# Layer 0's FFN, last F-tile: the context tokens' output groups and norms between the block products, head 0's weight remainders and half of the rope tables on VectorE

## The chip, the cores and the metric

One core of a Trainium2 chip runs the whole kernel. The metric is the device time of one execution in microseconds (us), as the median of several runs. The engines are TensorE (PE; its weight loads are PEld), VectorE (DVE), ScalarE (ACT), GpSimd (POOL) and the queue of SyncE (SP), which issues most transfers.

## The reference, cut to what matters

Two transformer layers over 512 latent tokens and 256 context tokens of width 1024. Each layer is a mixer (attention) and a SwiGLU FFN, each behind an RMS norm with a scale and shift, and each added to the stream through a gate row. The change is at the end of layer 0's FFN and the start of layer 1's mixer:

```
def _swiglu(h, w_in, w_out):
    gate, up = jnp.split(h @ w_in, 2, axis=-1)
    return (jax.nn.silu(gate) * up) @ w_out

x = x + gx2 * _swiglu(_rms(x, norm_ffn_w[l]) * (1.0 + scx2) + shx2, ffn_w_in[l], ffn_w_out[l])
ctx = ctx + gc2 * _swiglu(_rms(ctx, norm_ffn_w[l]) * (1.0 + scc2) + shc2, ffn_w_in[l], ffn_w_out[l])
# layer 1 (differential attention):
hx = _rms(x, norm_mix_w[l]) * (1.0 + scx1) + shx1      # the same for ctx
q, k, v = jnp.split(hx @ w_in, [qs, 2 * qs], axis=-1)  # q, k normed, and turned by rope for latent tokens
```

The FFN's hidden width is 2816, 22 F-tiles of 128.

## The kernel before, in words

Every fp32 matmul is done in three passes of the reduced type fp32r: each operand is split into a rounded part (hi, a cast on ACT) and a remainder (lo, a subtraction on DVE or POOL), and hi x hi, hi x lo, lo x hi are summed in PSUM. Names that end in h and l are these two parts: `wbh`/`wbl` blocks of FFN input weights, `wdh`/`wdl` output ("down") weights, `hdh`/`hdl` hidden rows, `wih`/`wil` layer 1's input weights, `hT` and `hTc` the normed tokens of the latents and the context, transposed.

Tokens are in six tiles of 128: 0 to 3 are latent, 4 and 5 context; `x0` to `x5` are their stream rows. `CTX_FIRST` is the order 4, 5, 0, 1, 2, 3.

`ffn_mixed` is layer 0's FFN. Its F-tiles f = 2 to 10 go through `by_blocks`. For the latents an F-tile is a fast 2 x 2 block scheme of seven products (r2, r1, r3, a11, a12, a22, r4; a product is 12 matmuls of 256 columns into `pu` or `pg`), whose weight blocks r1 to r4 are sums of the weights' four quarters (`ws`, made on POOL from the loaded `wr`). For the context the same tile takes plain gate and up products of the quarters (`gate_up`, 2 x 24 matmuls into `cgu`). `hi` and `lo` split the next weight blocks, in the order of the list `names`; the lo parts of r1 and r2 are on POOL, the others on DVE. Between the products stand groups: a group is the down product of one token tile and half of the 1024 outputs (9 matmuls of 512 columns into `dps` for three F-tiles), added to `x` by DVE. The context's groups of F-tiles 8 to 10 and the latents' all stand after the last F-tile, in the order CTX_FIRST.

What an earlier phase put into `x` was saved to DRAM. `gate(i)` makes a gate row: a transpose (`gps`), a copy (`grow`) on DVE, two DMAs. `resumed(t, eng)` loads a token tile's saved rows (`xr`) into one of two shared buffers ("raw"), multiplies `x` by the gate row and adds `xr`, on the engine given. `residual` multiplies a finished group by the gate row and adds it to `x`, both on DVE. `done(t)` is `norm_steps`: a square on ACT, an rsqrt and a scaling on POOL (`nh`), eight transposes on PE (`npt`), eight affine steps on DVE and ACT in turns (`nhc`), the split into `hT` or `hTc`.

Layer 1 works head by head. `in_proj1` loads a head's weights in four units through the raw buffers (`wir`), splits them (`by_pieces` is the subtraction in three pieces on POOL) and projects the six token tiles (`inps`, 24 matmuls each); `rotate_all` applies the rope tables `rt`, which `head_tables` makes on POOL; `kpt` and `qpt` are transposes of keys and queries. The split weights have five buffers and a head needs four.

Engines run their queues in order. The order is set by a list scheduler that models time, except in `ffn_mixed`, where `Pinned` engines keep the order in which the code is written, and where `tc.issue_after` holds an instruction behind another.

Of the kernel before, what the change touches and what calls it, by code (L numbers as in the profile page):

```python
# [18 lines left out]
P = 128  # L19
D = 1024  # L20
# [42 lines left out]
def backbone(es: ExitStack, tc: tile.TileContext, x, c, ctx, c_ctx, mod_w, mod_b, norm_mix_w, norm_ffn_w,  # L63
# [98 lines left out]
    def rsqrt(ss, n, inv, tag):  # L162

        r = small.tile([P, n], F32, name="rs_" + tag, tag="rs_" + tag)
        nc.gpsimd.tensor_scalar(r, ss, inv, EPS, ALU.mult, ALU.add)
        nc.gpsimd.tensor_tensor(r, r, neghalf[:, :n], ALU.pow)
        return r
# [78 lines left out]
    def norm_steps(t, xt, l, f, pool, tags=(("nh", 2), ("nhc", 2)), room=None):  # L246
# [8 lines left out]
        nc.scalar.activation(h, xt, AF.Square, accum_out=ss)  # L255
        r = rsqrt(ss, 1, 1.0 / D, "n")
        nc.gpsimd.tensor_scalar(h, xt, r, 1.0, ALU.mult, ALU.mult)
        yield
        hc = hc() if callable(hc) else hc
        hi, lo = tile_T(0, t), tile_T(1, t)  # L260
        for g in range(2):
            pt = tr_tile("npt", [P, 4, P])
            for k in range(4):
                nc.tensor.transpose(pt[:, k, :], h[:, 4 * g + k, :], ident)
            for k in range(4):
                kk = 4 * g + k
                a, c = aff[l][:, f, kk, i:i + 1], modc[l][:, 3 * f, kk, i:i + 1]
                if k % 2:
                    nc.scalar.activation(hc[:, kk, :], pt[:, k, :], AF.Identity, bias=c, scale=a)
                else:  # L270
                    nc.vector.tensor_scalar(hc[:, kk, :], pt[:, k, :], a, c, ALU.mult, ALU.add)
            ks = slice(4 * g, 4 * g + 4)
            nc.scalar.copy(hi[:, ks], hc[:, ks])
            nc.vector.tensor_sub(lo[:, ks], hc[:, ks], f32(hi[:, ks]))
# [51 lines left out]
    def head_tables(pool, wq, wk, nq, nk, w, rp):  # L326
# [10 lines left out]
        for j, h0, m in ((0, 0, nq), (1, nq, nk)):  # L337
            nc.vector.tensor_copy(wc[:, h0:h0 + m], bc(w[:, 0, j, :], 1, m))
            for i in range(2):
                wj = bc(bc(w[:, i, j, :], 1, m), 1, 2)  # L340
                for u in range(2):
                    nc.gpsimd.tensor_tensor(tb[u][:, :, i, h0:h0 + m], bc(rp[:, 2 * u:2 * u + 2, i, :], 2, m), wj,
                                            ALU.mult)
# [45 lines left out]
    def project(ps, t, ws, c0, c1):  # L389

        hs = [tile_T(j, t) for j in range(2)]
        for k in range(KT):
            whi, wlo = ws[k // 2]
            a, b = whi[:, k % 2, c0:c1], wlo[:, k % 2, c0:c1]
            nc.tensor.matmul(ps, hs[0][:, k, :], a, start=k == 0, stop=False)  # L395
            nc.tensor.matmul(ps, hs[0][:, k, :], b, start=False, stop=False)  # L396
            nc.tensor.matmul(ps, hs[1][:, k, :], a, start=False, stop=k == KT - 1)  # L397
# [174 lines left out]
    def in_proj1(h, tabs, wp, st, wh, qp):  # L572
        wc, tb = tabs
        ws = []
        for u in range(4):
# [5 lines left out]
            ws.append(unit(wh, views, [P, 2, 384], 5, "wi", None if h < 2 and u % 2 else by_pieces))  # L581
# [5 lines left out]
        for t in CTX_FIRST:  # L587
# [4 lines left out]
            with behind(nc.tensor) if h == 0 and t >= NTX else ExitStack():  # L592
                project(ps, t, ws, 384 - n, 384)
# [593 lines left out]
    def ffn_mixed(xs, w_down, w_up, fp, turn_over, new_rows, done, after):  # L1187
# [144 lines left out]
        names = ("r2", "r1", "r3", "a11", "a12", "a22", "a21", "r4")  # L1332

        class Weights:

            def __init__(self, f):
# [8 lines left out]
                todo.extend((self, n) for n in names)  # L1345
# [239 lines left out]
        def by_blocks(f, w, nxt, after, last, own):  # L1585
# [34 lines left out]
            if f == NF - 1:  # L1620
                gates[0] = gate(0, lambda *a, **kw: fp.tile(*a, tag="t1h", **kw))
# [22 lines left out]
            if f == NF - 1:  # L1644
# [39 lines left out]
            if f == NF - 1:  # L1684
                end(back[0])
                back[2] = resumed(2, pool)
                end(back[2])
# [9 lines left out]
            if f == NF - 1:  # L1697
                end(back[1])
                back[3] = resumed(3, pool)
                end(back[3])  # L1700
# [21 lines left out]

        w, nxt = w2, w3
        for f in range(2, NF):
# [206 lines left out]
    def done0(t):  # L1931
# [6 lines left out]
        return norm_steps(t, xs[t], 1, 0, None, room=room)  # L1938
# [216 lines left out]
```

## Time and profile before

| | us |
|---|---|
| median of 3 runs (1761.33 to 1769.43) | 1764.95 |
| the profiled execution | 1762.82 |
| its span, first to last instruction | 1760.9 |
| PE busy / POOL busy / DVE busy | 1672.6 / 1049.4 / 1192.4 |
| layer 0's last F-tile: first block product | 947.1 |
| layer 1, head 0: first projection matmul | 999.8 |

Times of instructions are us from the start of the span. In a row of the profile the line is that of kernel.py; the pinned instructions of the FFN all have one line, L765 (the wrapper), so they are told apart by their tiles. A group's row ends in "busy us, mean ns of one | idle time of the engine before them, and what ended it".

### The profile page before, as it was taken

The numbers are of one execution on the slowest core, as the hardware profiler recorded it, in microseconds if no ns is written. First come the engines' busy times: TensorE is split into PE (matmuls) and PEld (weight loads), VectorE is DVE, ScalarE is ACT, GpSimd is POOL, SyncE is SP. The second block draws the span as 40 slices with busy tenths as digits, with TensorE's granted clock in tenths as the row PEclk, the third lists the DMA queues.
The fourth block names the chain that finished last, engine by engine and source line by source line (L and its number), as shares of the span: only waits on it lengthen the run. The fifth ranks groups of instructions, "written<-read, shape, count | busy, mean of one in ns | idle before, by whom it ended". The sixth has DMA issues, their size and how long they took to land.

```text
span 1760.9 us, 30531 instructions
## 1 busy us (share of the span) xinstructions
PE 1672.6 (95%) x11322; PEld 1484.8 (84%) x11322; DVE 1192.4 (68%) x2181; ACT 915.1 (52%) x2030; POOL 1049.4 (60%) x1337
## 2 busy tenths in 40 slices
PE   5999999989899999999999889999998999999998
PEld 3887787667799998899989789999986788999997
DVE  4775555444768767877787765666665488777777
ACT  6556565533436555555553565666665355444441
POOL 2753332422647877788776766667773247777770
PEclk8999999999999999999999999999999999999999
DMA  9212233314343544454543311111122325333332
GB/s 311 63 44 73 82 99 101 128 49 124 104 132 120 157 155 144 133 166 146 155 126 125 123 37 37 36 38 37 48 94 84 96 73 167 94 94 102 108 96 96
DMA packets 206836, 184.79 MB, mean 105 GB/s; under 512 B 17056, under 2 KB 191712, under 8 KB 206688
## 3 DMA queue, kind: packets, MB, share of 16 engines
q1 hardware_dynamic: 205760, 180.55, 33.6%
q8 instruction: 89, 1.46, 0.3%
q10 hardware_dynamic: 928, 2.30, 0.3%
q14 instruction: 59, 0.48, 0.1%
HBM read 173.36 MB, written 9.46 MB: 104 GB/s over the span
## 4 chain that ended last, share of the span: by engine, by line
PE 69%; DVE 7%; POOL 7%; ACT 5%; DMA 5%; issue 3%; SPq 1%; ACTq 0%; POOLq 0%; DVEq 0%
PE dps L765 15%; PE pg L765 11%; PE pu L765 9%; PE cgu L765 5%; PE inps L395 3%; PE inps L396 3%; PE inps L397 3%; PE av L546 2%; PE sc L501 2%; PE ops L718 2%; POOL wil L286 2%; PE ops L720 2%; PE ops L719 2%; PE ppt L528 2%; PE av L666 1%
## 5 line engine op out<-in xcount | busy, mean ns | idle before, releaser
L765 DVE TENSOR_TENSOR x<-x,dps 128x512 f32<-128x512 f32 x268 | 176.4, 678 | 24.5 <-PE dps L765 24.0
L765 POOL TENSOR_TENSOR wbl<-ws,wbh 128x256 fp32r<-128x256 f32 x152 | 122.6, 837 | 105.0 <-PE pu L765 54.0
L765 PE MATMUL dps<-wdh,hdh 128*128 128x512 f32 x434 | 174.8, 403 | 8.1 <-DVE x L765 4.9
L765 PE MATMUL pg<-hT,wbh 128*128 128x256 f32 (+1 forms) x944 | 176.2, 284 | 2.4 <-DVE pg L765 1.6
L765 PE MATMUL dps<-wdl,hdh 128*128 128x512 f32 x434 | 172.2, 397 | 0.0
L765 PE MATMUL dps<-wdh,hdl 128*128 128x512 f32 x434 | 171.7, 396 | 0.3 <-DVE hdl L765 0.3
L765 ACT ACTIVATE modw<-modw,cols 128x256 f32<-128x256 f32 x256 | 109.4, 498 | 114.2 <-DMA modw<-in_mod_w_dram 103.2
L765 PEld LDWEIGHTS pg<-hT,wbh 128*128 128x128 f32 x944 | 150.8, 188 | 11.8 <-DVE pg L765 1.8
L765 POOL TENSOR_TENSOR modw<-modw 128x512 f32<-128x512 f32 (+1 forms) x96 | 119.7, 1247 | 64.9 <-ACT modw L765 59.2
L765 POOL TENSOR_TENSOR ws<-wr 128x256 f32<-128x256 f32 x152 | 145.4, 977 | 17.6 <-DMA wr<-in_ffn_w_in_dram 13.8
L395 PE MATMUL inps<-wih,hT 128*128 128x384 f32 x384 | 133.2, 347 | 0.9 <-ACT qkv L595 0.6
L765 PE MATMUL pg<-hT,wbl 128*128 128x256 f32 (+1 forms) x472 | 133.7, 283 | 0.0
L397 PE MATMUL inps<-wih,hT 128*128 128x384 f32 x384 | 131.1, 341 | 0.0
L396 PE MATMUL inps<-wil,hT 128*128 128x384 f32 x384 | 130.9, 341 | 0.0
L765 DVE TENSOR_TENSOR wbl<-wr,wbh 128x512 fp32r<-128x512 f32 x142 | 121.5, 859 | 5.9 <-ACT wbh L765 5.4
L765 PE MATMUL cgu<-hTc,wbh 128*128 128x256 f32 x640 | 114.2, 279 | 0.0
L765 ACT CAST wbh<-ws 128x512 fp32r<-128x512 f32 x152 | 87.3, 623 | 43.5 <-PE pg L765 31.6
L765 ACT CAST wbh<-wr 128x512 fp32r<-128x512 f32 x142 | 87.1, 619 | 37.3 <-PE pg L765 21.0
L765 PEld LDWEIGHTS cgu<-hTc,wbh 128*128 128x128 f32 x640 | 99.9, 188 | 3.4 <-issue 0.4
L765 PEld LDWEIGHTS dps<-wdh,hdh 128*128 128x128 f32 x434 | 81.9, 189 | 23.8 <-DVE x L765 8.4
L765 PEld LDWEIGHTS dps<-wdh,hdl 128*128 128x128 f32 x434 | 82.0, 189 | 20.2 <-DVE hdl L765 0.7
L765 PEld LDWEIGHTS dps<-wdl,hdh 128*128 128x128 f32 x434 | 82.2, 189 | 9.5
(388 smaller groups left out, 5270.7 us busy)
## 6 DMA issues: line engine op xcount, KB each, us to landing
modw<-in_mod_w_dram SPq DMA_DIRECT2D x108, 512.0 KB, 4.3
wr<-in_ffn_w_in_dram SPq DMA_DIRECT2D x84, 512.0 KB, 5.1
wdr<-in_ffn_w_out_dram SPq DMA_DIRECT2D x44, 512.0 KB, 3.7
wir<-in_od_w_in_dram SPq DMA_DIRECT2D x96, 128.0 KB, 2.3
x<-in_x_dram SPq DMA_DIRECT2D x8, 512.0 KB, 8.8
wir<-in_ev_w_in_dram SPq DMA_DIRECT2D x16, 256.0 KB, 2.8
wor<-in_ev_w_out_dram SPq DMA_DIRECT2D x8, 512.0 KB, 3.6
out_dram<-x SPq DMA_DIRECT2D x8, 512.0 KB, 2.6
```

What stands on the lines that cost most here:

```text
L286: nc.gpsimd.tensor_sub(lo[c], raw[c], hi[c])
L395: nc.tensor.matmul(ps, hs[0][:, k, :], a, start=k == 0, stop=False)
L396: nc.tensor.matmul(ps, hs[0][:, k, :], b, start=False, stop=False)
L397: nc.tensor.matmul(ps, hs[1][:, k, :], a, start=False, stop=k == KT - 1)
L501: nc.tensor.matmul(sc[:, s0:s0 + c1 - c0], q, kT[:, j, c0:c1], start=j == 0, stop=bool(j and last))
L528: nc.tensor.transpose(pt[:, h, :], Pt[h][:, cs], ident)
L546: mm = nc.tensor.matmul(av[64 * j:64 * j + 64, :], vv[:, vt[kc], :], P4[:, j::2, kc * P:(kc + 1) * P], start=i == 0, stop=i == nk - 1)
L666: nc.tensor.matmul(av, PT[:, a, :], vv[:, vt[kc], :], start=kc == 0, stop=kc == NT - 1)
L718: nc.tensor.matmul(ps, ohi[:, k, :], a, start=k == first, stop=False)
L719: nc.tensor.matmul(ps, ohi[:, k, :], b, start=False, stop=False)
L720: self.at = nc.tensor.matmul(ps, olo[:, k, :], a, start=False, stop=k == last)
L765: return tc.keep_in_program_order(op(*args, **kw))
```

## The change

The last F-tile leaves `by_blocks` for a function of its own, `last_tile`. There the context's gate and up come first, so that its hidden rows are ready early; the four context groups stand between the block products, each followed by its residual on DVE; tile 4's whole norm and the scaling of tile 5 stand before product r4. Gate row 0 is made after product r1; x0's saved rows are taken in on POOL and not on DVE, x1's on DVE, in the code behind r4. The list of weight blocks has another order for this tile. After it the latents' groups follow in the order 0 to 3, with two more PSUM banks in turn. The norms behind the FFN are pinned too.

In layer 1 all four units of head 0 are split on DVE (before: two on POOL); head 1's units 1 and 2 get two buffers in another pool; head 1's context projections may be issued after head 0's tile 1; four of the eight rope table products are on DVE.

The diff, cut to its core:

```diff
+    def norm_steps(t, xt, l, f, pool, tags=(("nh", 2), ("nhc", 2)), room=None,
+                   engs=(nc.tensor, nc.vector, nc.scalar, nc.gpsimd)):
...
+        def table(u, eng):
+            for j, h0, m in parts:
+                for i in range(2):
+                    eng.tensor_tensor(tb[u][:, :, i, h0:h0 + m], bc(rp[:, 2 * u:2 * u + 2, i, :], 2, m),
+                                      bc(bc(w[:, i, j, :], 1, m), 1, 2), ALU.mult)
+
+        table(0, nc.vector)
+        with tc.high_priority(-150):
+            table(1, nc.gpsimd)
...
-            ws.append(unit(wh, views, [P, 2, 384], 5, "wi", None if h < 2 and u % 2 else by_pieces))
+            pool, n = (wo, 2) if h == 1 and u in (1, 2) else (wh, 5)
+            ws.append(unit(pool, views, [P, 2, 384], n, "wi", None if h == 0 or h == 1 and u % 2 else by_pieces))
...
-            with behind(nc.tensor) if h == 0 and t >= NTX else ExitStack():
-                project(ps, t, ws, 384 - n, 384)
+            with tc.issue_after(first_head[0].ins) if h == 1 and t >= NTX else ExitStack():
+                mm = project(ps, t, ws, 384 - n, 384, Pinned(nc.tensor) if h == 0 and t >= NTX else nc.tensor)
+            if h == 0 and t == 1:
+                first_head.append(mm)
...
         names = ("r2", "r1", "r3", "a11", "a12", "a22", "a21", "r4")
+        last_names = ("a11", "a12", "a21", "a22", "r2", "r1", "r3", "r4")
...
-                todo.extend((self, n) for n in names)
+                todo.extend((self, n) for n in (names if f < NF - 1 else last_names))
...
-            if f == NF - 1:
-                gates[0] = gate(0, lambda *a, **kw: fp.tile(*a, tag="t1h", **kw))
...
-                for i, eng in ((0, dve), (1, dve)):
-                    back[i] = resumed(i, eng)
-                    next(back[i])
...
+        def ctx_group(t, n):
+            ps = down_bank()
+            for f in fs:
+                down_part(ps, f, t, n, f == fs[0], f == fs[-1])
+            yield
+            acc = xs[t][:, n * 512:(n + 1) * 512]
+            dve.tensor_mul(ps, ps, gates[1][:, n * 512:(n + 1) * 512])
+            dve.tensor_add(acc, acc, ps)
+            if n:
+                norms.append(done(t, (pe, dve, act, pool)))
+                next(norms[-1])
+
+        def last_tile(f, w, last):
+            t = Tile(f, w)
+            dn = down(f)
+            next(dn)
+            hidden_tiles(f)
+            t.gate_up(0)
+            next(last)
+            hi()
+            lo()
+            t.gate_up(1)
+            rest = hidden(f, SEQ, TOK, t.both[:, 0], t.both[:, 1], ctx_room("sgc"))
+            next(rest)
+            end(last)
+            next(rest)
+            next(dn)
+            end(rest)
+            t.product("r2")
+            end(dn)
+            t.product("r1")
+            gates[0] = gate(0, lambda *a, **kw: fp.tile(*a, tag="t1h", **kw))
+            back[0], back[1] = resumed(0, pool), resumed(1, dve)
+            for i in range(2):
+                next(back[i])
+            gs = [ctx_group(t, n) for t in CTX_FIRST[:2] for n in range(2)]
+            t.product("r3")
+            next(gs[0])
+            t.product("a11")
+            end(gs[0])
+            t.four()
+            end(back[0])
+            next(gs[1])
+            t.product("a12")
+            end(gs[1])
+            dve.tensor_add(t.a, t.a, t.q)
+            next(gs[2])
+            t.product("a22")
+            end(gs[2])
+            dve.tensor_add(t.e, t.e, t.u)
+            next(gs[3])
+            end(gs[3])
+            back[2] = resumed(2, pool)
+            end(back[2])
+            end(norms.pop(0))
+            t.product("r4")
+            end(back[1])
+            dve.tensor_add(t.c, t.c, t.v)
+            last = hidden(f, 0, SEQ, t.ps[1], t.ps[0], t.quv[:, :SEQ])
+            next(last)
+            back[3] = resumed(3, pool)
+            end(back[3])
+            return last
...
-        order = [(t, n) for t in CTX_FIRST for n in range(2)]
+        last = last_tile(NF - 1, w, last)
+        order = [(t, n) for t in range(NTX) for n in range(2)]
...
-            ps = open_[i] if i < 4 else acc_tile("dps", one=i % 2)
+            ps = open_[i] if i < 4 else new_bank(i)
```

How the instructions stand now, at three places. POOL, in F-tiles 9 and 10, before. (`wbl` from `ws` are the lo parts of r2 and r1, two pieces each; the `x4` and `x5` rows are the context's saved rows being taken in; `g1` is the context's gate row.)

```order
L765 TENSOR_TENSOR ws_10927<-wr_10605,wr_10607 128x256 x2
L765 TENSOR_TENSOR wbl_10944<-ws_10850,wbh_10943 128x256 x2
L765 TENSOR_TENSOR wbl_10965<-ws_10818,wbh_10964 128x256 x2
L765 TENSOR_TENSOR ws_11018<-wr_10605,ws_10850 128x256 x2
L765 TENSOR_TENSOR x4_4682<-x4_4682,g1_11014 128x1024
L765 TENSOR_TENSOR x4_4682<-x4_4682,xr_11016 128x1024
L765 TENSOR_TENSOR x5_4763<-x5_4763,g1_11014 128x1024
L765 TENSOR_TENSOR x5_4763<-x5_4763,xr_11080 128x1024
```

POOL there now:

```order
L779 TENSOR_TENSOR ws_10927<-wr_10605,wr_10607 128x256 x2
L779 TENSOR_TENSOR ws_11016<-wr_10605,ws_10850 128x256 x2
L779 TENSOR_TENSOR x4_4682<-x4_4682,g1_11012 128x1024
L779 TENSOR_TENSOR x4_4682<-x4_4682,xr_11014 128x1024
L779 TENSOR_TENSOR x5_4763<-x5_4763,g1_11012 128x1024
L779 TENSOR_TENSOR x5_4763<-x5_4763,xr_11078 128x1024
L779 TENSOR_TENSOR wbl_11083<-ws_10850,wbh_11082 128x256 x2
L779 TENSOR_TENSOR wbl_11101<-ws_10818,wbh_11100 128x256 x2
L779 TENSOR_TENSOR x0_4046<-x0_4046,g0_11265 128x1024
```

The lo parts of r2 and r1 have moved behind the four operations on `x4` and `x5`, and x0 comes to POOL.

DVE before, at the end of the last F-tile: the last products' sums (`pg`, `pu`), x0 and x1 taken in among them, then the hidden rows (`hdl`).

```order
L765 TENSOR_TENSOR pg_11164<-pg_11164,quv_11239 128x256
L765 TENSOR_TENSOR x0_4046<-x0_4046,g0_11202 128x1024
L765 TENSOR_TENSOR x0_4046<-x0_4046,xr_11223 128x1024
L765 TENSOR_TENSOR pu_11163<-pu_11163,quv_11239 128x256
L765 TENSOR_TENSOR x1_4203<-x1_4203,g0_11202 128x1024
L765 TENSOR_TENSOR x1_4203<-x1_4203,xr_11225 128x1024
L765 TENSOR_TENSOR cgu_11247<-sgc_11272,cgu_11247 128x256
L765 TENSOR_TENSOR hdl_11246<-cgu_11247,hdh_11245 128x256
L765 TENSOR_TENSOR pg_11164<-pg_11164,quv_11239 128x256
L765 TENSOR_TENSOR pu_11163<-quv_11239,pu_11163 128x512
L765 TENSOR_TENSOR hdl_11246<-pu_11163,hdh_11245 128x512
```

DVE there now, from the second lo half of tile 4's norm (`hTc1`) to the hidden rows:

```order
L779 TENSOR_TENSOR hTc1_4657<-nhc_11340,hTc0_4656 128x4x128
L779 TENSOR_SCALAR nhc_11340<-npt_11408,aff1_109,modc1_107 128x128 x2
L779 TENSOR_TENSOR hTc1_4657<-nhc_11340,hTc0_4656 128x4x128
L779 TENSOR_TENSOR x1_4203<-x1_4203,g0_11265 128x1024
L779 TENSOR_TENSOR x1_4203<-x1_4203,xr_11269 128x1024
L779 TENSOR_TENSOR pg_11164<-pg_11164,quv_11307 128x256
L779 TENSOR_TENSOR pu_11163<-quv_11307,pu_11163 128x512
L779 TENSOR_TENSOR hdl_11168<-pu_11163,hdh_11167 128x512
L779 TENSOR_SCALAR nhc_11386<-npt_11470,aff1_109,modc1_107 128x128
L302 TENSOR_TENSOR wil_11700<-wir_11695,wih_11699 128x768
```

x1 now stands directly ahead of the last sum on `pg`, behind tile 4's norm, and the first weight remainder (`wil`) follows the hidden rows.

DVE right after this, before: the residuals of the first four groups, all of them the context's.

```order
L402 TENSOR_TENSOR dps_11353<-dps_11353,g1_11014 128x512
L402 TENSOR_TENSOR dps_11354<-dps_11354,g1_11014 128x512
L403 TENSOR_TENSOR x4_4682<-x4_4682,dps_11353 128x512
L402 TENSOR_TENSOR pu_11355<-pu_11355,g1_11014 128x512
L403 TENSOR_TENSOR x4_4682<-x4_4682,dps_11354 128x512
L402 TENSOR_TENSOR pg_11356<-pg_11356,g1_11014 128x512
L403 TENSOR_TENSOR x5_4763<-x5_4763,pu_11355 128x512
L403 TENSOR_TENSOR x5_4763<-x5_4763,pg_11356 128x512
```

And now, the latents' (PSUM bank `pu` is free again after the last row, tile 1's first half being in `pu_11441`):

```order
L411 TENSOR_TENSOR dps_11439<-dps_11439,g0_11265 128x512
L779 TENSOR_SCALAR nhc_11386<-npt_11470,aff1_109,modc1_107 128x128
L412 TENSOR_TENSOR x0_4046<-x0_4046,dps_11439 128x512
L411 TENSOR_TENSOR dps_11440<-dps_11440,g0_11265 128x512
L412 TENSOR_TENSOR x0_4046<-x0_4046,dps_11440 128x512
L411 TENSOR_TENSOR pu_11441<-pu_11441,g0_11265 128x512
L302 TENSOR_TENSOR wil_11708<-wir_11703,wih_11707 128x768
L779 TENSOR_TENSOR hTc1_4657<-nhc_11386,hTc0_4656 128x4x128
L779 TENSOR_SCALAR nhc_11386<-npt_11481,aff1_109,modc1_107 128x128
L411 TENSOR_TENSOR pg_11442<-pg_11442,g0_11265 128x512
L302 TENSOR_TENSOR wil_11716<-wir_11711,wih_11715 128x768
L412 TENSOR_TENSOR x1_4203<-x1_4203,pu_11441 128x512
```

Two weight remainders, a norm's remainder and two affine steps stand among the residuals.

More of the change, by code (lines that the diff above doesn't have):

```diff
@@ L160, in backbone, with rsqrt @@
     sel2 = cst[:, C_S2:C_S2 + 2]
-    def rsqrt(ss, n, inv, tag):
+    def rsqrt(ss, n, inv, tag, eng=nc.gpsimd):
         r = small.tile([P, n], F32, name="rs_" + tag, tag="rs_" + tag)
-        nc.gpsimd.tensor_scalar(r, ss, inv, EPS, ALU.mult, ALU.add)
-        nc.gpsimd.tensor_tensor(r, r, neghalf[:, :n], ALU.pow)
+        eng.tensor_scalar(r, ss, inv, EPS, ALU.mult, ALU.add)
+        eng.tensor_tensor(r, r, neghalf[:, :n], ALU.pow)
         return r
@@ L268, in norm_steps @@
                 if k % 2:
[L269 removed]
+                    act.activation(hc[:, kk, :], pt[:, k, :], AF.Identity, bias=c, scale=a)
                 else:
[L271 removed]
+                    dve.tensor_scalar(hc[:, kk, :], pt[:, k, :], a, c, ALU.mult, ALU.add)
             ks = slice(4 * g, 4 * g + 4)
[L273 to L274 removed]
+            act.copy(hi[:, ks], hc[:, ks])
+            dve.tensor_sub(lo[:, ks], hc[:, ks], f32(hi[:, ks]))
     def norm_hT(*args, **kw):
@@ L1721, in by_blocks @@
             return last, own
+        fs = tuple(range(NF - 3, NF))
+        norms = []
+        def ctx_group(t, n):
[60 more added lines that the diff above has]
+            return last
         w, nxt = w2, w3
-        for f in range(2, NF):
+        for f in range(2, NF - 1):
             after = Weights(f + 2) if f + 2 < NF else None
@@ L1727, in ffn_mixed, with new_bank @@
             w, nxt = nxt, after
-        fs = tuple(range(NF - 3, NF))
-        order = [(t, n) for t in CTX_FIRST for n in range(2)]
-        open_ = [p_1.tile([P, 512], F32, name="dps", tag=f"acc{i}") for i in range(2)] + \
-            [banks.tile([P, SEQ], F32, name=n, tag=n) for n in ("pu", "pg")]
+        last = last_tile(NF - 1, w, last)
+        order = [(t, n) for t in range(NTX) for n in range(2)]
+        def new_bank(i):
+            return p_1.tile([P, 512], F32, name="dps", tag=f"acc{i % 2}") if i in (0, 1, 6, 7) else \
+                banks.tile([P, SEQ], F32, name=("pu", "pg")[i % 2], tag=("pu", "pg")[i % 2])
+        open_ = [new_bank(i) for i in range(4)]
         for ps, (t, n) in zip(open_, order):
@@ L1735, in ffn_mixed @@
         end(last)
-        norms = []
+        end(norms.pop(0))
         for i, (t, n) in enumerate(order):
-            ps = open_[i] if i < 4 else acc_tile("dps", one=i % 2)
+            ps = open_[i] if i < 4 else new_bank(i)
             for f in fs[2 * (i < 4):]:
                 down_part(ps, f, t, n, f == fs[0], f == fs[-1])
-            residual(xs[t], ps, gates[t >= NTX], n)
+            residual(xs[t], ps, gates[0], n)
             if n:
```

46 lines of the change are left out of this document (18 added, 28 removed).

## The prediction

> **What bounds the kernel now.** I read the head and busy shares of the page first, then PE's waits from 947 us (the start of layer 0's last F-tile) to the third head of layer 1, then a table of stretches of that time.
>
> ```profile
> span 1760.9 us, 30531 instructions
> PE 1672.6 (95%) x11322; PEld 1484.8 (84%) x11322; DVE 1192.4 (68%) x2181; ACT 915.1 (52%) x2030; POOL 1049.4 (60%) x1337
> ```
>
> TensorE is the bound over the whole span, so a change that keeps its matmuls can win only where it stands still. Stretches: length, then busy us of PE, PEld, DVE, ACT, POOL, then PE's granted clock.
>
> ```profile
> 947.00:964.00 17.00, 16.16 (x136) 15.97 (x136) 13.70 (x20) 4.20 (x8) 7.96 (x3) 1.00 0.37 125
> 979.00:1000.00 21.00, 16.47 (x76) 12.84 (x75) 17.46 (x32) 13.94 (x29) 14.81 (x19) 0.92 0.52 169
> 1014.00:1032.00 18.00, 15.03 (x88) 13.95 (x87) 12.67 (x28) 13.55 (x33) 12.23 (x22) 0.91 0.03 8
> 1032.00:1045.00 13.00, 10.45 (x66) 9.27 (x65) 6.15 (x14) 7.97 (x20) 9.45 (x17) 0.87 0.39 111
> 1074.00:1084.00 10.00, 7.09 (x45) 6.54 (x43) 2.53 (x6) 4.20 (x13) 8.32 (x16) 0.83 0.29 83
> ```
>
> PE idles 0.8, 4.5, 3.0, 2.6 and 2.9 us here, 13.8 in all, and where it idles the clock falls too. In the second row DVE is busy 17.5 of 21 us: it is the engine that PE waits for. The waits by name (total, times, longest):
>
> ```profile
> PE npt L264 <- ACT nhc L269: 3.6, 2, 2.3
> PE kpt L622 <- ACT o L269: 2.4, 1, 2.4
> PE inps L396 <- POOL wil L286: 2.1, 1, 2.1
> PE inps L395 <- ACT wih L299: 1.2, 1, 1.2
> PE pg L765 <- DVE quv L765: 0.8, 1, 0.8
> ```
>
> The first is the tail of the FFN, the second tile 2's norm behind head 0's projections, the wil and wih rows the weights of heads 1 and 2.
>
> **The change, part by part.** TensorE's own work is as before; its pieces in the chain (start, us):
>
> ```profile
> 851.44 1.44 PE pu L765 x12
> 852.88 1.39 PE dps L765 x6
> 862.73 2.80 PE cgu L765 x24
> ```
>
> *The last tile's start.* Gate and up of the context now come first, at the place of r2's first matmul (947.1, below): two of 2.80, to 952.7. Then r2 and r1 are wanted, but their lo parts stand on POOL behind context's four row operations, which wait for gate row 1.
>
> ```profile
> 936.21 0.27 DVE L765 COPY grow<-gps 8x128 f32<-8x128 f32 x1
> 941.80 2.39 POOL L765 TENSOR_TENSOR x<-x,g 128x1024 f32<-128x1024 f32 x1 [2.82 <-DMA g<-gmem]
> 949.88 2.75 POOL L765 TENSOR_TENSOR x<-x,xr 128x1024 f32<-128x1024 f32 x1
> L765 POOL TENSOR_TENSOR wbl<-ws,wbh 128x256 fp32r<-128x256 f32 x4 | 2.9, 754 | 0.6 <-PE dps L765 0.6
> ```
>
> The four end at 952.6; the copy of the row starts about 1.2 later than at 936.21, since DVE now does two lo parts ahead of it, so they end at 953.8, and the first half of r2's lo 0.75 later, 954.5. r2's third matmul wants it at 952.9, so PE waits 1.6 (0 if DVE has slack for the two, 2.5 if they also collide with POOL). The 0.8 behind DVE quv goes, since a group now runs while q is copied; I keep it as slack within these bounds.
>
> *The groups between products.* Where PE stood and where head 0 begins:
>
> ```profile
> 947.07 0.28 PE L765 MATMUL pu<-t2h,wbh 128*128 128x256 f32 x1
> 999.84 0.36 PE L395 MATMUL inps<-wih,hTc 128*128 128x256 f32 x1
> ```
>
> From 954.3 (952.7 and 1.6): three products 4.3, four groups of nine (1.5 x 1.40) 8.4, three products 4.3, eight transposes 0.8 (an estimate, half of six 512-column matmuls and a start), r4 1.4: 973.5. The 24 matmuls of tiles 0 and 1 that need no new hidden rows take 5.6, tile 5's transposes 0.8: at 979.9 PE wants the last tile's latent hidden rows. What hides the groups' own follow-up (eight residual halves, 0.69 and 0.68) is DVE's idle time in this stretch, 13.7 busy of 17; without it each pair would cost 1.4.
>
> *Gate row 0 and x0.* The row is now made after r1 and not ahead of r3, its copy queued behind the last down weights' lo parts, near 957.9 instead of 952.03 (context's hidden rows, the cast of the down weights and their lo parts come first, an estimate of 5.2 after 952.7); it fills POOL's wait 6.5 later, at 964.3. x0 moves from DVE to POOL (two of 2.4, to 969.1), and context tile 4's scaling queues behind it (to 971.1), which is when PE wants tile 4's transposes (971.3). So x0 costs nothing, with nothing to spare; were the row 2 later, PE would wait those 2.
>
> ```profile
> 952.03 0.27 DVE L765 COPY grow<-gps 8x128 f32<-8x128 f32 x1
> xr<-out_dram SPq DMA_DIRECT2D x4, 512.0 KB, 3.6
> wir<-in_od_w_in_dram SPq DMA_DIRECT2D x32, 128.0 KB, 2.3
> ```
>
> *Loads on SP.* Two raw buffers serve the saved rows of x0 to x3 and then head 0's weights, in order. x3's rows now wait for x2's add (981.1), unit u0 for x1's add (985.9 below, before 969.2), unit u1 for x3's add: u0 lands near 989.0 (three issues and 2.3), u1 near 991.
>
> *Those rows are late.* On DVE they now stand behind context tile 4's norm and behind x1's multiply and add. Here POOL's multiply and a DVE operation with two SBUF inputs exclude each other:
>
> ```profile
> 958.49 2.41 POOL L765 TENSOR_TENSOR x<-x,g 128x1024 f32<-128x1024 f32 x1 [5.87 <-DMA g<-gmem]
> 958.76 3.23 DVE L765 TENSOR_TENSOR x<-x,g 128x1024 f32<-128x1024 f32 x1
> 963.50 1.21 DVE L765 TENSOR_TENSOR x<-x,g 128x1024 f32<-128x1024 f32 x1
> 967.09 0.42 DVE L765 TENSOR_TENSOR pg<-pg,quv 128x256 f32<-128x256 f32 x1
> 969.58 0.69 DVE L765 TENSOR_TENSOR hdl<-pu,hdh 128x512 fp32r<-128x512 f32 x1 [0.65 <-ACT hdh L765]
> L255 ACT ACTIVATE nh<-x 128x1024 f32<-128x1024 f32 x4 | 4.2, 1060 | 4.7 <-DVE x L403 4.1 <-DVE nhc L271 0.6
> L257 POOL TENSOR_SCALAR nh<-x,rs_n 128x1024 f32<-128x1024 f32 x4 | 4.5, 1124 | 0.4
> ```
>
> With POOL free the multiply takes 1.21; issued 0.27 after POOL's it took 3.23, POOL's rest and its own 1.2. Group (5, 1) ends at 971.3, x5 is done at 972.5; ACT squares it (1.06) ahead of tile 4's affines and casts, so DVE's second lo part for tile 4 is wanted at 977.1 (972.5, the square and its readout 1.2, then affines and casts by turns on both engines 3.4, an estimate). POOL has scaled x5 by 975.7 (square 1.2, its rsqrt 0.8, scaling 1.12) and goes on with x2 and x3, each 2.41. By turns: POOL to 978.1, lo part to 978.7, POOL to 981.1, x1 multiply to 982.3, POOL to 984.7, x1 add to 985.9. From pg's add to the hdl part is 2.49 (967.09 to 969.58), so hidden rows are there at 988.3 and PE waits 8.4. I take the turns, since the 3.23 row is the same operation on the same tiles. Bounds: 2.4 if DVE never waits for POOL, 9.5 if x5's scaling collides too.
>
> [...]
>
> *The banks.* Tile 2's first group reuses tile 1's bank, freed by x1's first residual add. DVE's fifteen steps from the hidden rows up to it:
>
> ```profile
> L402 DVE TENSOR_TENSOR dps<-dps,g 128x512 f32<-128x512 f32 x10 | 6.9, 693 | 3.0 <-PE dps L765 2.9
> L403 DVE TENSOR_TENSOR x<-x,dps 128x512 f32<-128x512 f32 x10 | 6.7, 679 | 0.1
> L271 DVE TENSOR_SCALAR nhc<-npt,aff,modc 128x128 f32<-128x128 f32 x16 | 5.9, 402 | 0.7 <-ACT nhc L269 0.5
> L274 DVE TENSOR_TENSOR hT<-nhc,hT 128x512 fp32r<-128x512 f32 x2 | 1.4, 684 | 0.0
> 978.26 0.96 DVE L300 TENSOR_TENSOR wil<-wir,wih 128x768 fp32r<-128x768 f32 x1 [1.56 <-ACT wih L299]
> ```
>
> Three weight lo parts (0.96), seven residual halves (0.69), hdl and one hT lo (0.68), three affines (0.40): 10.3, less 0.07 a step by which neighbours overlap (the sixteen affines of 0.402 make 6.4, their busy time is 5.9, eight pairs), 9.3, and 0.4 in which u0 is not yet cast (989.0 and 0.8): from 988.4 to 998.1. PE's twelve matmuls end at 991.1: it waits 7.0, of which the weights are 2.9 (before, u0 and u2 were on POOL). The second bank is freed one multiply, one affine and one add after the first group, 1.6 more. Bounds for both 4 to 10: DVE's work alone, or u1 a whole load later. From 998.1: groups 4.2 and 4.2, waiting 1.6, transposes twice 0.8: head 0's first projection at 1009.7. Before, it came at 999.8: **+9.9**.
>
> *Rope tables.* Half of the eight go to DVE, beside head 0's projections (the second row is for the rival on POOL below).
>
> ```profile
> L342 POOL TENSOR_TENSOR rt<-rp,rw 128x256 f32<-128x256 f32 x8 | 6.3, 809 | 0.1
> L286 POOL TENSOR_TENSOR wil<-wir,wih 128x256 fp32r<-128x256 f32 x9 | 8.9, 1013 | 1.9 <-ACT wih L299 1.9
> ```
>
> POOL loses four x 0.81. Tile 2's transposes still stand directly ahead of its projection, so of the 2.4 wait I take 1.5 off: **-1.5** (0 to -3; a pair on DVE hidden under head 0's 14 us of projections; were that cover gone, 1.7).
>
> *Pinned norms and the new bank order* issue the same instructions; they cost nothing beyond the queues above.
>
> *Heads 1 and 2.* Units 1 and 2 of head 1 get buffers of their own, and part of its projection comes before tile 2's. Before, they waited for head 0's buffers:
>
> ```profile
> SPq L292 <- ACT wih L299: 54.9, 5, 26.6
> 994.00:996.00 2.00, 2.00 (x6) 1.52 (x6) 0.85 (x3) 1.26 (x4) 1.83 (x4) 0.50 0.22 88
> ```
>
> In the two stretches of heads 1 and 2 PE idles 2.6 and 2.9 and loses half of a spell at clock 0.5 (clock shares 0.87 and 0.83: 13 x 0.13 and 10 x 0.17, 1.7 each). I keep 0.5 and 0.8 for the last unit, which still waits for a buffer: **-3.8 and -3.8** (0 to -4.6 each). POOL's pieces for head 2 move ahead with them and lie beside projections, if POOL has the time.
>
> [...]
>
> **Sum:** 9.9 - 1.5 - 3.8 - 3.8 = +0.8. The profiled execution took 1762.82 (span 1760.9, 1.9 around it), 2.1 under the median 1764.95 of the runs; it becomes 1763.6, the median 1765.7.
>
> **Rivals.**
> - *The tail becomes bound by PE* (faster). For it: context's 8.4 us of groups leave a stretch in which DVE was at 83%. It needs x1 done by 977.5, ahead of POOL's x2, and wil parts that wait for nothing; then the second stretch's losses go (4.5 idle, 21 x 0.08 = 1.7 of clock), the 1.6 at the tile's start stays, and the projection comes 4.6 earlier, not 9.9 later: -4.6 - 9.1 = -13.7, 1751. Against it: the order of DVE's queue.
> - *POOL takes the heads' gain back* (slower). Head 2's three units, nine pieces of about 1.0, now stand among the rotations that head 0 and 1 wait for; a unit ahead of a rotation costs 3.0. If the 7.6 is not won and one unit is paid: 9.9 - 1.5 + 3.0 = +11.4, 1776. For it: POOL is busy 9.5 of 13 and 8.3 of 10 us in those two stretches. It decides, with the unit paid, once less than 2.6 of the 7.6 is left. Against: these pieces are the same number as before, only earlier.
> - *DVE is not held up by POOL at x1*: PE's first wait is 2.4 and not 8.4, the sum 6.0 less, -5.2, 1760. For it: POOL might be late itself, behind the gate row's DMA. Against: the 3.23 row.
> - *The clock spells have another cause than these waits* and come anyway: 1.7 twice stays, +4.2, 1769. For it: the waits in heads 1 and 2 are short, 2.1 at most. Against: the 0.50 row lies behind waits hardly longer. [...]
> - *Nothing moves* cannot be: PE's order differs at the tile's start.
>
> **Numbers.** Forecast 0.45, PE-bound tail 0.22, POOL 0.17, no hold-up 0.11, spells 0.05. Under 0.5% (8.8 us) a measurement of this kernel hardly tells a change from none. So faster 0.22, same 0.61, slower 0.17. The likeliest alone reaches from 1758 to 1773; 8 in 10 needs half of each outer rival, 1751 to 1776.
>
> **What would show it.** PE waits of over 6 us before the last tile's dps (releaser ACT hdh) and near 5 before pu dps (releaser DVE x) show the two stalls; x1's multiply or add at over 2 us on DVE shows the hold-up; no wait on wih or wil in head 1 or 2 shows the gain. A projection that starts before 1000 breaks the forecast, as does a tail that stands still for the gate row's DMA (5.87 before, on POOL).

## The result, and the profile after

| | runs | median, us | ratio to before, 95% interval |
|---|---|---|---|
| before | 14 | 1763.95 (1761.33 to 1769.43) | |
| changed | 14 | 1774.26 (1768.37 to 1779.36) | 1.0053 (1.0041 to 1.0064) |

The change makes the kernel slower, by 0.53% or 9.3 us by the ratio of the runs (the medians differ by 10.3). That lies inside the range of the prediction (1751 to 1776), but outside the likeliest case's own (1758 to 1773), and 8.6 us above the forecast; by the prediction's line at 0.5% it is the outcome 'slower', to which it gave 0.17. The profiled execution took 1775.22. The head of its page:

```profile
span 1773.4 us, 30532 instructions
PE 1676.7 (95%) x11322; PEld 1486.2 (84%) x11322; DVE 1192.7 (67%) x2185; ACT 915.3 (52%) x2030; POOL 1047.5 (59%) x1329
```

The engines' work is as it was; the time went into standing still. PE's waits from the start of the last F-tile to head 0's first projection, then in heads 0 to 2 (total, times, longest):

```profile
PE dps L779 <- ACT hdh L779: 9.5, 1, 9.5
PE npt L779 <- ACT nhc L271: 1.7, 1, 1.7
PE npt L779 <- ACT nhc L779: 0.9, 1, 0.9
PE npt L779 <- POOL nh L259: 0.8, 1, 0.8
PE npt L779 <- POOL nh L779: 0.7, 1, 0.7
PE pu L779 <- POOL wbl L779: 0.5, 1, 0.5
...
PE inps L403 <- ACT qkv L609: 3.7, 3, 1.6
PE kpt L636 <- ACT o L271: 1.4, 1, 1.4
```

One wait of 9.5 us for the last hidden rows stands out, as forecast. There is no row `pu <- DVE x`, which the forecast had put near 5. In heads 1 and 2 no wait on `wih` or `wil` is left, but the single wait on `qkv` (0.8 before) has become three (3.7). The stretches (length, busy us of PE, PEld, DVE, ACT, POOL, then PE's granted clock):

```profile
949.90:966.90 17.00, 16.43 (x119) 15.40 (x120) 10.28 (x17) 3.84 (x8) 8.69 (x7) 1.00 0.41 128
983.70:993.20 9.50, 0.02 (x1) 0.00 (x0) 8.15 (x6) 1.18 (x2) 5.20 (x3) 0.77 0.29 85
993.20:998.50 5.30, 5.29 (x13) 4.10 (x14) 4.23 (x8) 2.55 (x5) 0.00 (x0) 0.50 0.71 198
1014.40:1032.00 17.60, 17.60 (x127) 17.14 (x125) 12.55 (x29) 9.64 (x23) 13.56 (x24) 1.00 0.27 80
1032.00:1052.00 20.00, 16.21 (x111) 15.12 (x110) 13.01 (x27) 15.01 (x36) 14.67 (x22) 1.00 0.15 41
```

The second row is the stall: PE does one matmul in 9.5 us while DVE is busy for 8.2. The third is what follows it: 5.3 us at half clock. Head 0's projections (fourth row) then run without a gap, where before PE was busy for 15.0 of 18 us. In the fifth row (the end of head 0's part and head 1's projections) PE idles 3.8 of 20 us, and the clock is 1.00 all the same.

To compare traces, I weigh each matmul by the median time from the start of one of its shape to the next (0.23 us for 512 columns, 0.17 for 384, 0.12 for 256), and ask how much later than in the kernel before the same amount of work is reached. This is called lateness below, in us:

| at | changed |
|---|---|
| F-tile 9, near 932 us | 1.6 |
| last F-tile's start | 2.7 |
| head 0's first projection | 14.6 |
| the middle of head 2, near 1100 | 9.3 |
| head 4, near 1210 | 11.7 |
| the end of layer 1's mixer | 11.2 |
| end | 12.5 |

The first 1.6 arise before anything is changed; in the other traces of this document the lateness there, behind the same code, lies between -1.1 and 1.6. How the matmuls are weighed can shift a figure by up to 1 us more. The tail costs 13.0, heads 0 to 2 give 5.3 back, and at the start of head 4 another 2.5 go. The last 1.3 are discussed at the end.

### The profile page after: what moved, and what is told of

It is laid out like the page before. It is cut to its first block, busy times and chain, and to the rows that moved or that the text cites. A ratio compares the mean times of both kernels' runs of the same rounds, so it can differ in the third digit from the quotient of the medians.

```text
span 1773.4 us, 30532 instructions
## 1 busy us (share of the span) xinstructions
PE 1676.7 (95%) x11322; PEld 1486.2 (84%) x11322; DVE 1192.7 (67%) x2185; ACT 915.3 (52%) x2030; POOL 1047.5 (59%) x1329
## 4 chain that ended last, share of the span: by engine, by line
PE 70%; DVE 7%; POOL 6%; ACT 5%; DMA 4%; issue 3%; SPq 0%; ACTq 0%; POOLq 0%; DVEq 0%
PE dps L779 15%; PE pg L779 11%; PE pu L779 9%; PE cgu L779 5%; PE inps L403 3%; PE inps L404 3%; PE inps L405 3%; PE av L555 2%; PE sc L510 2%; DMA modw<-in_mod_w_dram 2%; PE ops L732 2%; PE ops L734 2%; POOL wil L288 2%; PE ops L733 2%; PE ppt L537 2%
## 5 line engine op out<-in xcount | busy, mean ns | idle before, releaser
L779 PE MATMUL dps<-wdh,hdh 128*128 128x512 f32 x428 | 173.0, 404 | 15.9 <-ACT hdh L779 10.7
L779 DVE TENSOR_TENSOR wbl<-wr,wbh 128x512 fp32r<-128x512 f32 x142 | 116.2, 823 | 6.6 <-ACT wbh L779 6.3
L779 PEld LDWEIGHTS pg<-hT,wbl 128*128 128x128 f32 x472 | 88.9, 188 | 0.7
```

Of the source, the lines that this page charges most:

```text
L779: return tc.keep_in_program_order(op(*args, **kw))
```

## Experiments

The theory from this trace: x1's take-in, held up by POOL, makes the hidden rows late; the tail's loss is the result, and layer 1's parts give some of it back. The first four kernels take these apart.

**The FFN alone, and layer 1 alone.** The first has the new `last_tile`, its norms and banks, with `head_tables`, `in_proj1` and its call as before; the second has the former FFN and takes over those three:

```diff
+        table(0, nc.vector)
+        with tc.high_priority(-150):
+            table(1, nc.gpsimd)
...
+            pool, n = (wo, 2) if h == 1 and u in (1, 2) else (wh, 5)
+            ws.append(unit(pool, views, [P, 2, 384], n, "wi", None if h == 0 or h == 1 and u % 2 else by_pieces))
```

> The changed FFN (last F-tile, its groups, norms and bank order) with layer 1 as it was before: head 0's units 0 and 2 split on POOL, no buffers of their own for head 1, all rope tables on POOL. Theory (the loss is made in the FFN's tail, and layer 1's parts give back a part of it): without what they give back, about 5 of the 14.6 us by which head 0's first projection was late in the changed kernel, and with 2.9 won because two weight remainders leave DVE, the median is 1772 to 1778, ratio to before 1.005 to 1.008. Rival (layer 1's parts cost time too, the waits of heads 1 and 3 behind ACT and POOL are theirs): 1766 to 1771, ratio 1.001 to 1.004.

> The FFN as before with layer 1's parts of the change: all four of head 0's remainders on DVE, two buffers of their own for head 1, head 1's context projections allowed earlier, half of the rope tables on DVE. Theory (these parts are a gain by themselves, some 3 to 6 us): 1758 to 1761.5, ratio 0.9965 to 0.9985. Rival (they are worth nothing where the tail is not late, since what heads 1 and 2 win is paid in head 1's waits behind ACT and in head 3's behind POOL): 1763 to 1768, ratio 0.9995 to 1.002.

The FFN alone: 1771.99, ratio 1.0037 (1.0025 to 1.0048). The median is just under the theory's range, the ratio inside the rival's, so the run does not decide between them. Layer 1 alone: 1770.25, 1.0027 (1.0016 to 1.0039), slower than before, which neither theory nor rival had. Its lateness tells why: -1.0 at head 0's first projection, -9.9 in the middle of head 2, then +0.8 at head 4 and +8.1 at the end of the mixer. Layer 1's parts win about as much as the prediction gave them, 11 us from the last F-tile's start, and lose 18 in heads 3 to 7, where the change has no line. Waits of PE there, layer 1 alone (1085 to 1330 us):

```profile
PE inps L402 <- POOL wil L286: 11.8, 5, 3.1
PE inps L401 <- ACT qkv L607: 2.0, 2, 1.8
```

In the kernel before, the same stretch has no wait on `wil`.

**x1's saved rows on POOL.**

```diff
-            back[0], back[1] = resumed(0, pool), resumed(1, dve)
+            back[0], back[1] = resumed(0, pool), resumed(1, pool)
...
+            end(back[1])
             back[2] = resumed(2, pool)
...
             t.product("r4")
-            end(back[1])
```

> The changed kernel with x1's saved rows taken in on POOL, ahead of x2's, and not on DVE. Theory (the hidden rows are late because x1's two operations stand before them on DVE and each take 3.3 us beside POOL's): the wait for the last hidden rows falls from 9.5 to about 3 us, head 0's first projection comes 5 to 6.6 us earlier, median 1767 to 1770, ratio to before 1.002 to 1.004. Rival (the wait only moves: POOL now ends x3 about 3 us later, so the raw buffer of weight unit 1 comes free later and the banks take what the hidden rows give): the first projection moves less than 2 us, median 1772 to 1775.

Median 1770.18, 0.2 above the theory's range, ratio 1.0029 (1.0018 to 1.0040), inside it. The wait for the hidden rows is 2.9 and not 9.5, and head 0's first projection is reached at a lateness of 6.5, 5.9 of it since F-tile 9 (13.0 in the changed kernel):

```profile
PE dps L779 <- ACT hdh L779: 2.9, 1, 2.9
```

So the stall is x1's place and time on DVE. But of 7 us won up to head 0 the median keeps 4: heads 0 to 2 then give back 2.7 and not 5.3. They recover less when there is less to recover.

**POOL idle beside x1.** The first attempt only moved x2's and x3's operations behind the hidden rows in the code.

```diff
-            end(back[2])
+            next(back[2])
...
         end(last)
+        end(back[2])
+        back[3] = resumed(3, pool)
+        end(back[3])
```

> The changed kernel with x1 on DVE at its place, but POOL's x2 and x3 only after the hidden rows, so that POOL is idle while DVE does the last lo part of tile 4's norm and x1's multiply and add. Theory (POOL holds DVE up): those three operations, 2.83, 3.36 and 3.25 us in the changed kernel, take 0.7, 1.2 and 1.2, and the wait for the hidden rows falls from 9.5 to 3 to 4 us. Rival (their place in the queue is what costs, not the hold-up): they stay above 2 us each, and the wait stays above 7. In both, x2 and x3 come later and with them weight unit 1, so the median says less than the wait: 1768 to 1778.

Median 1775.91; the wait stayed at 9.6, and so did the three durations (2.85, 3.35, 3.32). This tells nothing on the question: POOL's queue holds nothing between tile 5's scaling and x2, so x2 still started at 976.5. In code that is written in order, an instruction moved past an empty stretch of its own queue has not moved. The second attempt gives x2 and x3 to DVE:

```diff
-            back[2] = resumed(2, pool)
-            end(back[2])
+            back[2] = resumed(2, dve)
+            next(back[2])
...
-            back[3] = resumed(3, pool)
-            end(back[3])
+            back[3] = resumed(3, dve)
+            next(back[3])
...
         end(last)
+        end(back[2])
+        end(back[3])
```

> The changed kernel with x2's and x3's saved rows taken in on DVE, behind the last hidden rows, and not on POOL, so that POOL is really idle beside tile 4's last lo part and x1's multiply and add (the earlier run that was to do so left POOL where it was, since its queue had nothing else). Theory (POOL's operations hold DVE's up): those three take 0.7, 1.2 and 1.2 us where they took 2.83, 3.36 and 3.25, and the wait for the hidden rows is 3 to 4 us and not 9.5. Rival (the place in DVE's queue is the cost): above 2 us each, wait above 7. The four operations now stand among the residuals, which costs up to 4.8 us again: median 1768 to 1775.

DVE's rows in the changed kernel, and then POOL's at the same time (start, duration):

```profile
978.32 0.69 DVE L779 TENSOR_TENSOR hTc<-nhc,hTc 128x512 fp32r<-128x512 f32 x1 [1.18 <-ACT hTc L779]
...
981.45 2.83 DVE L779 TENSOR_TENSOR hTc<-nhc,hTc 128x512 fp32r<-128x512 f32 x1 [1.18 <-ACT hTc L779]
984.20 3.36 DVE L779 TENSOR_TENSOR x<-x,g 128x1024 f32<-128x1024 f32 x1
987.59 3.25 DVE L779 TENSOR_TENSOR x<-x,xr 128x1024 f32<-128x1024 f32 x1
...
978.44 2.84 POOL L779 TENSOR_TENSOR x<-x,g 128x1024 f32<-128x1024 f32 x1
981.36 2.37 POOL L779 TENSOR_TENSOR x<-x,xr 128x1024 f32<-128x1024 f32 x1
983.69 2.79 POOL L779 TENSOR_TENSOR x<-x,g 128x1024 f32<-128x1024 f32 x1
987.33 2.42 POOL L779 TENSOR_TENSOR x<-x,xr 128x1024 f32<-128x1024 f32 x1 [0.85 <-DMA xr<-out_dram]
```

And DVE with POOL idle, then the wait:

```profile
981.05 0.69 DVE L779 TENSOR_TENSOR hTc<-nhc,hTc 128x512 fp32r<-128x512 f32 x1 [1.18 <-ACT hTc L779]
981.66 1.22 DVE L779 TENSOR_TENSOR x<-x,g 128x1024 f32<-128x1024 f32 x1
982.92 1.22 DVE L779 TENSOR_TENSOR x<-x,xr 128x1024 f32<-128x1024 f32 x1
...
PE dps L779 <- ACT hdh L779: 3.2, 1, 3.2
```

The hold-up is shown: 9.44 us become 3.13, and the wait falls by 6.3, the same. The median, 1780.45 (ratio 1.0085, 1.0072 to 1.0098), is outside the expectation: x2 and x3 now delay x0's residual, tile 0's norm makes PE wait 4.4 and 3.0 us (releasers `nh` and `nhc`), and the later heads fell into an order with 8.1 us of waits on `wil`.

**Why heads 3 to 7 lose.** The five buffers are used in turn, so a head's weight unit takes the buffer of the unit ahead of it in the previous head. After TensorE's last use of that buffer, ACT casts (0.83) and POOL subtracts in three pieces (2.3), and the raw load needs another unit's subtraction to end first. The list scheduler decides how many matmuls of attention stand in between. I summed them from TensorE's program order, in the weights above. The least of units 1 to 3, for heads 2 to 7, in whole us (cut, not rounded), beside the waits on `wil` from head 2's middle on (about 1085 to 1330):

| kernel | head 2 | 3 | 4 | 5 | 6 | 7 | waits on wil | median |
|---|---|---|---|---|---|---|---|---|
| before | 6 | 7 | 7 | 7 | 7 | 7 | 0 | 1764 to 1765 |
| changed | 5 | 6 | 5 | 6 | 7 | 7 | 1.9 | 1774.26 |
| layer 1 alone | 5 | 6 | 6 | 6 | 6 | 6 | 11.8 | 1770.25 |

Where head 1 has buffers of its own, head 2's units take other buffers than the table counts for them, so only heads 3 to 7 are to be read in those rows.

The theory: where these distances are short, POOL's remainder comes too late, and edits of layer 1's first heads flip the order for all later ones. That can be tested without touching a later head, since every variant of the early parts lands in some order. The next five kernels have the FFN as before. First without the rope tables on DVE, then without the buffers:

```diff
-        table(0, nc.vector)
-        with tc.high_priority(-150):
-            table(1, nc.gpsimd)
...
+                for u in range(2):
+                    nc.gpsimd.tensor_tensor(tb[u][:, :, i, h0:h0 + m], bc(rp[:, 2 * u:2 * u + 2, i, :], 2, m), wj,
+                                            ALU.mult)
```

```diff
-            pool, n = (wo, 2) if h == 1 and u in (1, 2) else (wh, 5)
+            pool, n = wh, 5
```

> The FFN as before, layer 1's parts of the change without the rope tables (all eight products on POOL as before). With the tables on DVE this lost, from head 2 to head 6, all that it had won (11 us by head 2's end, then waits on wil of 2 to 3 us at every head). Theory (the later loss is the list scheduler's order: where it leaves TensorE only 5 or 6 us of matmuls between the last use of a weight buffer and the first use of the next unit in it, POOL's remainder comes too late; 7 us are enough): in this kernel only heads 2 and 4 have the short distance, so waits on wil are at most 5 us in all after head 2, and the median is 1757 to 1762. Rival (the early gain is given back whatever the order, since POOL has no time): waits on wil of 10 us or more, 1766 to 1772.

> The FFN as before, layer 1's parts of the change without the two own buffers of head 1's units. Theory (the short distances between uses of a weight buffer come from these buffers, which let the heads' order slip): waits on wil after head 2 under 2 us, the gains of DVE's remainders and tables stay, 1756 to 1761. Rival (the buffers are what wins, the rest is worth nothing): 1762 to 1766.

Without the rope tables: 1764.63, ratio 0.9995 (0.9985 to 1.0005), the same as before, between the two expectations; the one trace of it is of an execution that took 4153.57 us, and no waits are read from it. Without the buffers: 1761.41, ratio 0.9976 (0.9966 to 0.9986), faster than before, 0.4 above the theory's bound. Waits on `wil` after head 2 are 0.4. The distances are 6, 7, 6, 6, 7, 7, so 6 us alone do not bring the wait.

Then buffers for other units of head 1, chosen by the order they lead to (the kernel with units 1 and 3 also lacks the `tc.issue_after` ahead of head 1's context projections, and head 0's are ordered there as before the change; the third has units 2 and 3 and the tables on POOL):

```diff
-            pool, n = (wo, 2) if h == 1 and u in (1, 2) else (wh, 5)
+            pool, n = (wo, 2) if h == 1 and u in (1, 3) else (wh, 5)      # or (2, 3)
```

> The FFN as before; layer 1's parts of the change with the own buffers given to head 1's units 1 and 3 (and not 1 and 2), and without the rule that holds head 1's context projections behind head 0's tile 1. In its TensorE order at least 7 us of matmuls lie between the uses of a weight buffer at every head from 2 on, and heads 4 to 7 stand as before the change. Theory (the buffers win up to 10 us in heads 0 to 2, and the order alone decides if that is kept): no wait on wil over 1 us after head 2, median 1754 to 1760. Rival (POOL has no time whatever the order, and the gain goes): 1762 to 1768.

> The FFN as before; layer 1's parts of the change with the own buffers given to head 1's units 2 and 3. Its order has 6 to 8 us between the uses at head 2, and heads 3 to 7 stand as before the change, with 7 us. Theory (order decides): waits on wil after head 2 under 1 us, median 1754 to 1760, faster than the kernel before. Rival (no time on POOL): 1762 to 1768.

> As the kernel with buffers for units 2 and 3, but all rope tables on POOL as before the change. This flips the list scheduler's order from head 3 on: 5 or 6 us of matmuls between the uses of a weight buffer at every head from 3 to 7. Theory (order decides): waits on wil of 2 to 3 us at each of these heads, 8 to 14 us in all, median 1764 to 1770, slower than its twin by 6 us or more, though it differs from it in four products of 0.8 us alone. Rival (the order plays no part): within 3 us of its twin, waits on wil under 3 us in all after head 2.

| kernel | distances, heads 2 to 7 | waits on wil | lateness, head 2 / head 4 / mixer's end | median | ratio |
|---|---|---|---|---|---|
| units 1, 3 | 7 7 7 7 7 7 | 1.8 | -4.8 / -0.1 / -0.2 | 1760.19 | 0.9974 (0.9963 to 0.9985) |
| units 2, 3 | 6 7 7 7 7 7 | 0 | -9.8 / -10.5 / -10.0 | 1756.51 | 0.9956 (0.9940 to 0.9971) |
| units 2, 3, tables on POOL | 7 6 5 5 6 6 | 14.9 | -6.6 / +8.1 / +14.8 | 1780.25 | 1.0081 (1.0067 to 1.0095) |

Waits of PE from 1085 to 1330 us: the kernel with the tables on POOL, and behind the dots its twin with half of them on DVE, its first two rows:

```profile
PE inps L396 <- POOL wil L286: 14.9, 7, 3.1
PE inps L395 <- ACT wih L299: 2.4, 4, 1.3
...
PE inps L401 <- ACT qkv L607: 3.8, 6, 0.7
PE sc L651 <- ACT e L656: 1.5, 4, 0.7
```

The twins differ in where four products of 0.8 us run and in the priority that the scheduler gives the other four, and by 23.7 us in the median. The last kernel here was expected to be slow and was slower still; the one with units 2 and 3 is the fastest of all, 7.8 us under before. Units 1 and 3 landed 0.2 above the theory's bound and lost 4.6 us at head 3 in spite of 7 us of distance: three waits of 2.8 in all (1.8 on `wil`) and a spell of low clock behind them (granted 0.67 over 10 us). So a short distance at head after head goes with the large loss in every trace here, but 7 us are no guarantee, and 6 need not hurt. POOL's own order changes together with TensorE's, and no run here separates the two.

**The changed kernel with other buffers.** Finally two of these edits, no own buffers and buffers for units 2 and 3, as the only ones on the changed kernel:

> The changed kernel without the two own buffers of head 1's units. The order of heads 3 to 7 is then that of the kernel before, with 7 us of matmuls between the uses of a weight buffer. Theory (in the changed kernel the buffers win nothing, since the late tail hides head 1's and 2's weights anyway, and their order costs 2 to 4 us at heads 2 to 4): no wait on wil over 1 us after head 2, median 1769 to 1772.5. Rival (the buffers are worth the 3 to 8 us that the prediction gave them): 1776 to 1782.

> The changed kernel with the own buffers given to head 1's units 2 and 3 instead of 1 and 2, and nothing else. Its order keeps 7 us of matmuls between the uses of a weight buffer at every head from 3 on (the changed kernel has 5 or 6 at head 4). Theory (the changed kernel's loss is the FFN's tail, about 12 us up to head 0's first projection, of which heads 0 to 2 give back about 5, and order costs it another 2 to 4 us in later heads): no wait on wil over 1 us after head 2, the wait for the hidden rows still 9 to 10 us, median 1768 to 1772, still slower than the kernel before. Rival (with a good order the heads' gain of 10 us is free to pay for the tail): 1764 to 1767.

Without buffers: 1774.47, ratio 1.0052 (1.0037 to 1.0068), the changed kernel's own time, which neither expected; one wait on `wil` of 1.4 is left after head 2. So in the changed kernel the buffers are worth nothing, neither a gain nor a loss. With units 2 and 3: 1769.40, ratio 1.0028 (1.0015 to 1.0042), as the theory had it. The wait for the hidden rows is 8.9 (9 to 10 expected), none on `wil` is left after head 2, lateness is 9.7 at head 0's first projection, 2.4 in head 2 and 2.5 at head 4. It is still slower than before.

The medians side by side, by FFN and by layer 1's version:

| layer 1 | FFN before | FFN changed | difference |
|---|---|---|---|
| as before | 1764.6 | 1771.99 | 7.4 |
| buffers for units 1, 2 (the change) | 1770.25 | 1774.26 | 4.0 |
| no buffers | 1761.41 | 1774.47 | 13.1 |
| buffers for units 2, 3 | 1756.51 | 1769.40 | 12.9 |

These medians come from sessions whose own median of the kernel before ran from 1763.95 to 1765.33; by the ratios the differences are 6.5, 4.6, 13.4 and 12.7 us.

In the last row both orders keep their distances; there the FFN's own price is seen, 12.9 us, about what the tail adds up to head 0's first projection (13.0 in the changed kernel's trace, 10.7 in that with units 2 and 3). In the first row the old layer 1 hides 5 of it.

## Why the prediction was right, and where it was wrong

That the range held is in part luck. Its upper end came from half of the rival "POOL takes the heads' gain back", and the mechanism of that rival is not what the trace shows; the forecast's own mechanism ended at 1773. What was right is the stall ahead of the last hidden rows.

- **The late hidden rows: right.** Forecast 8.4 (2.4 to 9.5), measured 9.49, with x1's two operations at 3.36 and 3.25 where 'over 2' was named. The lo part of tile 4's norm was caught too (2.83, its twin 0.69). The run with POOL idle shows the hold-up, of the add as of the multiply: 3.36 and 3.25 become 1.22 each, and the lo part's 2.83 becomes 0.69.
- **The tail's start: size off.** r2's lo part costs 0.5, not 1.6; between F-tile 9 and the last F-tile's start another 1.1 go, 0.4 of it a wait of `cgu` on `modc` and 0.2 one of `dps` on `x`, both results of DVE; that the lo parts now ahead of them on DVE are the cause is a reading of the order, not tested. x0 had "nothing to spare": POOL's multiply began at 967.25, 2.9 after the forecast, of which 1.6 are the early lateness, and tile 4's transposes waited 0.7 for `nh`. The sign that was to break the forecast, a stand for the gate row's DMA, is there on POOL (8.58 ahead of that multiply), but those 0.7 are all that PE shows of it.
- **The banks: wrong in mechanism, right in size by luck.** No PE instruction waits for x1's first add. Tile 2's group is in `pu` at 998.50, while that add only starts at 1002.81:

```profile
998.50 0.63 PE L779 MATMUL pu<-wdh,hdh 128*128 128x512 f32 x1
...
1002.81 0.68 DVE L412 TENSOR_TENSOR x<-x,pu 128x512 f32<-128x512 f32 x1
```

  The pool behind `pu` and `pg` holds two tiles of each name (`bufs=2` in `block_banks`); I had read one. What fills the time is half clock behind the stall (granted 0.50; 2.8 us more than at full clock from 993 to 999, and 1.3 from 1006 to 1009) and the waits of the norms' transposes (the rows `npt` above). From the hidden rows to head 0's projection the forecast was 21.4 us and the trace shows 21.2. The sum of a stage can agree while no term in it does.
- **Rope tables and head weights: the step that failed.** The prediction took 9.1 us off, from the waits of the kernel before. Measured in the changed kernel: 5.3 by head 2, 2.9 after head 4's start. The wait of `kpt` on `o`, which the rope tables were to shorten by 1.5, went from 2.4 to 1.4, but with the tables left on POOL (the FFN alone) it is 1.8 already. The sign named for the gain, no wait on `wih` or `wil` in heads 1 and 2, is there, and 3.7 of waits on `qkv` beside it. Two things were wrong. First, these waits do not add in full to a late tail: with the new FFN and the old layer 1, heads 0 to 2 give back 3.6 of 13.5 by themselves, and of the old waits on `wih` and `wil` (3.9 in all there) 1.3 are left in heads 1 and 2, presumably because the loads run on while PE stands, which no run tests. Second, the edit changed the order of heads 1 to 5, and head 4 pays for it: one wait on `wil`, and lateness from 9.1 to 11.6. With buffers for units 2 and 3, heads 0 to 2 give back 7.3 behind the same late tail and keep it. The changed kernel's wait at head 4:

```profile
PE inps L404 <- POOL wil L288: 1.9, 1, 1.9
```

- **The rivals.** "POOL takes the heads' gain back" named 1776 and is nearest, and POOL is the engine; but it put the price at rotations of heads 0 and 1, while the trace has it at head 4's weights and, in layer 1 alone, in five waits on weights. The new waits in head 1 are ACT's: `qkv` behind a cast that waits for its load (1.6) and behind a load of an activation table (1.5; the load takes 1.28). The PE-bound tail and "no hold-up" are out, by the 9.5 row. The rival on the clock spells is out too, since the clock is 1.00 in both rows of heads 0 and 1 above. But the forecast's reason, that the spells go with the waits, is not shown by it: in head 1 waits of 1.6 and 1.5 are there and no spell follows.

## What to carry to other kernels

A gain that is read from waits downstream must be read again behind the loss upstream: with the FFN alone changed 1.3 us were left of 3.9 us of waits on weights, and a wait that is gone behind lateness cannot be won again. Under a list scheduler, an edit's largest price can lie a hundred us and more behind its lines: compare the whole later order, above all how much work stands between the last use of a buffer and the next use of its successor, before timing it. Three VectorE operations with two SBUF inputs took 2.83, 3.36 and 3.25 us beside GpSimd's multiplies and adds, and 0.69, 1.22 and 1.22 with GpSimd idle; an affine step that reads PSUM (979.86 in the changed kernel) kept its 0.41 beside them. Where such a collision threatens, keep an operation of the first kind that the critical path waits for away from GpSimd's large ones, by its place among GpSimd's work and not by its place in the code.

## What the hardware showed unexpectedly

At the start of layer 1's FFN PE has the same two waits in every trace, 1.2 and 0.9 us. Before, and in the changed kernel, over 8 us from about 1.5 us ahead of the first:

```profile
1403.00:1411.00 8.00, 5.84 (x46) 5.26 (x45) 7.31 (x14) 7.46 (x16) 2.82 (x3) 1.00 0.91 270
...
1414.00:1422.00 8.00, 5.84 (x33) 5.25 (x32) 7.32 (x14) 7.36 (x16) 2.82 (x3) 0.81 0.94 266
```

PE is busy for 5.84 us in both, but does 46 matmuls in one and 33 in the other, at clock 1.00 and 0.81. That is 1.5 of the last lateness in the table above. Of the thirteen traces that can be compared, seven show the spell and six do not: six of the seven with the changed FFN, and one of the six with the FFN before. So neither FFN fixes it, but that the change makes it likelier cannot be ruled out. What sets the spell off is not shown: the two waits are the same with it and without it. The spell also bounds how closely one trace can be set against another here: at this one place the same two waits cost 1.5 us more or not.
